# A low-rank-adapted linear layer: VectorE's point of resumption, the last chunk's load, and the placing of two programs

## The chip, the cores and the metric

The kernel runs on one core of one Trainium2 chip. The time is that of the device, in microseconds, for one execution. Five engines run their own instruction streams and meet at semaphores: PE (TensorE, matrix products), DVE (VectorE), ACT (ScalarE), POOL (GpSimd) and SP (SyncE, which here only issues transfers). Transfers between the chip's main memory and the core's on-chip memory (128 partitions) are carried by 16 DMA engines; a transfer that one queue issues is cut into packets that are spread over all 16.

## What is computed

A linear layer with a low-rank addition, on 32,768 rows of 256 numbers:

```
x_flat = x.reshape(-1, in_dim)              # 32768 x 256, fp32
y = x_flat @ W                              # W: 256 x 256
lora_out = x_flat @ lora_A                  # lora_A: 256 x 16
lora_out = lora_out * lora_E
lora_out = lora_out @ lora_B                # lora_B: 16 x 256
y = y + scale * lora_out
return y.reshape(batch, seq_len, out_dim).astype(np.float32)
```

x is 33.55 MB and so is the result; every byte of x is loaded once and every byte of the result stored once.

## The kernel before

The kernel first folds the low-rank part into the weights: `weff = W + A * (E * scale) * B`, kept in bf16. After that the layer is one product, x times `weff`.

**Chunks.** `PLAN` cuts the rows into five chunks: 56, 56, 48, 48 and 48 rows for each of 128 partitions. Three slots in on-chip memory hold them; chunk 3 goes into the slot of chunk 0 and chunk 4 into that of chunk 1. The result overwrites x in the slot, row by row, and a chunk is stored with one transfer when it is finished. `PIECES` says in how many transfers a chunk is loaded: three for chunks 0 and 1, two for chunks 2 and 3, one for chunk 4.

**Steps.** A step t is 8 rows per partition; there are 32. Steps 0 to 6 are chunk 0, 7 to 13 chunk 1, 14 to 19 chunk 2, 20 to 25 chunk 3, 26 to 31 chunk 4. Each step passes through four stages:
- `rounded(t)`, VectorE (L152): 128x2048 numbers of x from fp32 to bf16, into one of two `xb` buffers. It waits for the load of the piece where a piece begins.
- `transposed(k)`, PE (L191): eight transposes into `psum_xt`, with two bf16 numbers moved as one 32-bit word. Each adds to the semaphore `s_t` when the eight are done, so "s_t at 19" means that 19 steps have been transposed.
- `copied(t)`, VectorE (L156): `psum_xt` to on-chip memory.
- `multiplied(k)`, PE (L202): sixteen products of 128x256 into `psum_y`, in two halves; ScalarE evicts each half into the slot (L225).

**Order.** It is written out by hand. VectorE alternates: `copied(t)`, then `rounded(t + 2)`. PE alternates in a loop: the transposes of step t + 1, then the products of step t. So the products of a chunk's last step stand behind the transposes of the next chunk's first step.

**The queue.** All loads and stores of chunks are issued by SP on one queue, in this order: loads 0, 1, 2, then store 0, store 1, load 3, load 4, store 2, store 3, store 4. A load into a slot waits until the store out of it has landed (load 3 for store 0, load 4 for store 1). `ISSUE_STORE` and `ISSUE_LOAD` make some issues wait besides until `s_t` has reached a number: store 1 for 17, load 4 for 19, store 3 for 28. A store also waits for the chunk's last eviction.

**The hold.** `HOLD = 17, 1` keeps VectorE at the rounding of step 17 until store 1 has landed (L147 to L151). Ten NOPs stand in front of that wait:

```
        if t == HOLD[0]:
            for _ in range(10):
                nc.vector.engine_nop()
            nc.vector.wait_ge(s_st[HOLD[1]].sem, 16)
```

The lines that matter later: L104 issues every transfer, L150 is the NOPs, L152 the rounding, L236 and L241 are SP's waits on `s_t`, and the stretch ahead of `opening.append(...)`, where the new alignment goes in.

Of the kernel before, what the change touches and what calls it, by code (L numbers as in the profile page):

```python
# [3 lines left out]

PLAN = [56, 56, 48, 48, 48]

PIECES = {0: [16, 16, 24], 1: [16, 16, 24], 2: [24, 24], 3: [24, 24]}

SLOTS = [56, 56, 48]
LEAD = 3  # L10
AFTER = {1: [3, 4]}

HOLD = 17, 1

ISSUE_LOAD, ISSUE_STORE = {4: 19}, {1: 17, 3: 28}

S, G = 8, 4
P = 128
FP32 = mybir.dt.float32
BF16 = mybir.dt.bfloat16  # L20
# [15 lines left out]
def kernel(tc, x, W, lora_A, lora_B, lora_E, scale, out):  # L36
    nc = tc.nc
    x_flat = x.flatten_outer_dims()
    out_flat = out.flatten_outer_dims()
    N, K = x_flat.shape  # L40
# [14 lines left out]
    def sbuf(name, shape, dt):  # L55
        return nc.alloc_sbuf_tensor(name, shape, dt).ap()
# [9 lines left out]
    b_bf = sbuf("b_bf", [R, M], BF16)  # L66
    ate = sbuf("ate", [R, KC, P], BF16)
    weff = sbuf("weff", [P, KC, M], BF16)
    ident = sbuf("ident", [P, P], FP32)

    xb = [sbuf(f"xb{k}", [P, S, K], BF16) for k in range(2)]
# [13 lines left out]
    for i, b in enumerate(PLAN):  # L85
        parts = PIECES.get(i, [b])
        pieces[i] = [(sum(parts[:j]), n) for j, n in enumerate(parts)]
    s_ld = {(i, r): Count(nc, f"s_ld{i}_{r}") for i in pieces for r, n in pieces[i]}
    s_st = [Count(nc, f"s_st{i}") for i in range(len(PLAN))]
    s_id, s_set, s_v, s_t, s_m, s_y = (  # L90
        Count(nc, k) for k in ("s_id", "s_set", "s_v", "s_t", "s_m", "s_y"))


    can_m = nc.alloc_semaphore("can_m")
# [3 lines left out]
    def slot(i):  # L98
        return slots[i % LEAD][:, :PLAN[i], :]
# [20 lines left out]
        nc.tensor.wait_ge(sem, 1).then_inc(sem, -1)  # L120

    opening.append(tc.info.no_tile_sem_insts)
    transfer(nc.sync, s_w, out=w_sb, in_=W.rearrange("(p c) m -> p c m", c=KC))
# [7 lines left out]
    for i in range(1, LEAD):  # L133
# [5 lines left out]
        out=ident, in_=ident, compare_op=mybir.AluOpType.not_equal, fill=1.0, base=0,  # L139
# [3 lines left out]
    def rounded(t):  # L143
        i, r = steps[t]
        if (i, r) in s_ld:
            nc.vector.wait_ge(s_ld[i, r].sem, 16)
        if t == HOLD[0]:  # L147

            for _ in range(10):
                nc.vector.engine_nop()  # L150
            nc.vector.wait_ge(s_st[HOLD[1]].sem, 16)  # L151
        nc.vector.tensor_copy(out=xb[t % 2], in_=slot(i)[:, r:r + S, :]).then_inc(can_t[t % 2], 1)  # L152

    def copied(t):
# [8 lines left out]
    for c in range(KC):  # L163
# [5 lines left out]
        out=ate, in0=ps_at, scalar1=e_sb, scalar2=float(scale),  # L169
# [6 lines left out]
    nc.vector.wait_ge(s_set.sem, 2)  # L176
    s_v.by(nc.vector.tensor_add(out=weff, in0=w_sb, in1=ps_aeb))  # L177
    rounded(0)
    rounded(1)
    for t in range(NS):  # L180
        copied(t)
        if t + 2 < NS:
            rounded(t + 2)
# [105 lines left out]
```

## Time and profile before

| what | value |
|---|---|
| median of 3 runs | 161.82 us (161.81 to 161.85) |
| the profiled execution, its own time | 161.88 us |
| its span, first to last instruction | 160.6 us |
| bytes moved | 67.42 MB, mean 420 GB/s over the span |
| mean granted TensorE clock | 0.832 |

The transfers on SP's queue, by the trace's records of issue and of landing (each of the 16 DMA engines reports its share; the last report is shown):

| transfer | issued, us | landed, us |
|---|---|---|
| load 0, three pieces | 1.17 to 2.11 | 9.05, 13.95, 21.25 |
| load 1, three pieces | 3.33 to 4.43 | 26.14, 31.04, 38.34 |
| load 2, two pieces | 4.94, 5.43 | 45.65, 53.11 |
| store 0 | 34.66 | 70.44 |
| store 1 | 55.47 | 87.45 |
| load 3, two pieces | 70.46, 70.84 | 94.73, 102.03 |
| load 4, one piece | 94.65 | 116.57 |
| store 2 | 102.67 | 131.06 |
| store 3 | 124.55 | 146.06 |
| store 4 | 140.43 | 160.54 |

How to read it: a transfer is issued long before it lands, because it stands in line behind those issued earlier. The difference between the landings of two neighbours is what the later one needed for itself. The queue would run dry only if a transfer were issued after the one ahead of it had landed. "Span" leaves out 1.3 us that the execution's own time has around the first and last instruction. The page's parts are: engine totals, forty time slices, DMA queues, the chain of waits that ended last, and groups of instructions.

### The profile page before, as it was taken

The numbers are of one execution on the slowest core, as the hardware profiler recorded it, in microseconds if no ns is written. First come the engines' busy times: TensorE is split into PE (matmuls) and PEld (weight loads), VectorE is DVE, ScalarE is ACT, GpSimd is POOL, SyncE is SP. The second block draws the span as 40 slices with busy tenths as digits, with TensorE's granted clock in tenths as the row PEclk, the third lists the DMA queues.
The fourth block names the chain that finished last, engine by engine and source line by source line (L and its number), as shares of the span: only waits on it lengthen the run. The fifth ranks groups of instructions, "written<-read, shape, count | busy, mean of one in ns | idle before, by whom it ended". The sixth has DMA issues, their size and how long they took to land.

```text
span 160.6 us, 1871 instructions
## 1 busy us (share of the span) xinstructions
PE 93.9 (58%) x780; PEld 84.2 (52%) x780; DVE 76.5 (48%) x67; ACT 63.2 (39%) x65; POOL 0.7 (0%) x6
## 2 busy tenths in 40 slices
PE   0159979999999920000000899999569999700000
PEld 0039959999999910000000789999458999500000
DVE  0178679998989300000002968987094985000000
ACT  1101746867777640000000077777605586800000
POOL 1000000000000000000000000000000000000000
PEclk9999999999999997555555599999955999995555
DMA  5999999999999999999998999999999999999994
GB/s 158 426 433 451 435 408 433 449 441 404 459 410 392 457 459 457 457 457 443 443 414 347 404 453 429 435 529 404 404 392 478 465 429 392 416 478 441 416 404 196
DMA packets 2658, 67.42 MB, mean 420 GB/s; under 512 B 464, under 2 KB 480, under 8 KB 608
## 3 DMA queue, kind: packets, MB, share of 16 engines
q1 hardware_dynamic: 2448, 67.37, 97.7%
q10 hardware_dynamic: 208, 0.03, 0.3%
q14 instruction: 2, 0.02, 0.0%
HBM read 33.85 MB, written 33.55 MB: 420 GB/s over the span
## 4 chain that ended last, share of the span: by engine, by line
PE 36%; DMA 34%; DVE 2%; ACT 1%; issue 0%; SPq 0%
PE psum_y L202 23%; DMA out_dram<-xy 20%; DMA xy<-in_x_dram 14%; PE psum_xt L191 13%; DVE xb L152 2%; ACT xy L225 1%; SPq L241 0%; SPq L236 0%
## 5 line engine op out<-in xcount | busy, mean ns | idle before, releaser
L225 ACT COPY xy<-psum_y 128x1024 f32<-128x1024 f32 x64 | 61.9, 1017 | 73.7 <-PE psum_y L202 73.7
L202 PE MATMUL psum_y<-weff,xt 128*128 128x256 bf16 x512 | 64.4, 281 | 0.1
L191 PE MATMUL psum_xt<-ident,xb 128*128 128x128 f32 x264 | 38.1, 293 | 37.9 <-DVE xb L152 37.9
L152 DVE CAST xb<-xy 128x2048 bf16<-128x2048 f32 x32 | 38.9, 1219 | 41.4 <-DMA out_dram<-xy 33.5
L202 PEld LDWEIGHTS psum_y<-weff,xt 128*128 128x128 bf16 x512 | 51.8, 101 | 7.4 <-issue 0.3
L191 PEld LDWEIGHTS psum_xt<-ident,xb 128*128 128x128 f32 x264 | 33.1, 152 | 39.6 <-DVE xb L152 39.2
L156 DVE COPY xt<-psum_xt 128x1024 f32<-128x1024 f32 x32 | 39.1, 1222 | 10.4 <-PE psum_xt L191 10.3
L164 PE MATMUL psum_xt<-ident,a_sb 128*16 128x128 f32 x2 | 0.6, 394 | 4.2 <-POOL ident L138 4.2
L160 DVE CAST b_bf<-b_sb 16x256 bf16<-16x256 f32 x1 | 0.3, 280 | 5.4 <-DMA b_sb<-in_lora_B_dram 5.4
L225 ACT ACT_TABLE_LOAD x1 | 1.3, 1283 | 3.5 <-PEq L132 3.5
L173 PE MATMUL psum_xt<-b_bf,ate 16*128 16x256 bf16 x2 | 0.6, 403 | 3.2 <-DVE ate L168 3.2
L164 PEld LDWEIGHTS psum_xt<-ident,a_sb 128*16 128x16 f32 x2 | 0.1, 90 | 4.2 <-DMA a_sb<-in_lora_A_dram 4.2
L173 PEld LDWEIGHTS psum_xt<-b_bf,ate 16*128 16x128 bf16 x2 | 0.1, 105 | 3.7 <-DVE ate L168 3.7
L168 DVE TENSOR_SCALAR ate<-psum_xt,e_sb 16x256 bf16<-16x256 f32 x1 | 0.5, 471 | 1.8 <-DMA e_sb<-in_lora_E_dram 1.8
L177 DVE TENSOR_TENSOR weff<-w_sb,psum_xt 128x512 bf16<-128x512 f32 x1 | 0.7, 689 | 0.8 <-PE psum_xt L173 0.8
L138 POOL TENSOR_SCALAR_AFFINE_SELECT ident<-ident 128x128 f32<-128x128 f32 x1 | 0.3, 293 | 0.2 <-POOL ident L136 0.2
L136 POOL MEMSET ident<- 128x128 f32 x1 | 0.2, 205 | 2.9 <-POOLq L132 2.9
L270 POOL MEMSET const-bfloat16-1.0<- 128x1 bf16 x1 | 0.1, 102 | 0.0
L270 POOL MEMSET const-uint8-127<- 128x1 uint8 x1 | 0.1, 102 | 0.0
L270 POOL MEMSET const-float32-0.0<- 128x1 f32 x1 | 0.1, 99 | 0.2 <-issue 0.2
L270 POOL MEMSET const-float32-1.0<- 128x1 f32 x1 | 0.1, 99 | 0.0
## 6 DMA issues: line engine op xcount, KB each, us to landing
xy<-in_x_dram SPq DMA_DIRECT2D x6, 3072.0 KB, 32.5
out_dram<-xy SPq DMA_DIRECT2D x3, 6144.0 KB, 21.5
out_dram<-xy SPq DMA_DIRECT2D x2, 7168.0 KB, 33.9
xy<-in_x_dram SPq DMA_DIRECT2D x4, 2048.0 KB, 17.6
xy<-in_x_dram SPq DMA_DIRECT2D x1, 6144.0 KB, 21.9
w_sb<-in_W_dram SPq DMA_DIRECT2D x1, 256.0 KB, 2.8
a_sb<-in_lora_A_dram ACTq DMA_DIRECT2D x1, 16.0 KB, 3.0
b_sb<-in_lora_B_dram ACTq DMA_DIRECT2D x1, 16.0 KB, 4.2
```

The costliest lines, as they stand in the source:

```text
L138: s_id.by(nc.gpsimd.affine_select(out=ident, in_=ident, compare_op=mybir.AluOpType.not_equal, fill=1.0, base=0, pattern=[[-1, P]], channel ...
L152: nc.vector.tensor_copy(out=xb[t % 2], in_=slot(i)[:, r:r + S, :]).then_inc(can_t[t % 2], 1)
L156: nc.vector.tensor_copy(out=xt[t % 2], in_=ps_xt[t % 2]).then_inc(can_m, 1)
L160: s_v.by(nc.vector.tensor_copy(out=b_bf, in_=b_sb))
L164: at_done = nc.tensor.transpose(ps_at[:, c, :], a_sb[:, c, :], ident)
L168: s_v.by(nc.vector.tensor_scalar(out=ate, in0=ps_at, scalar1=e_sb, scalar2=float(scale), op0=mybir.AluOpType.mult, op1=mybir.AluOpType.mult))
L173: aeb_done = nc.tensor.matmul(ps_aeb[:, c, :], ate[:, c, :], b_bf, start=True, stop=True)
L177: s_v.by(nc.vector.tensor_add(out=weff, in0=w_sb, in1=ps_aeb))
L191: done = nc.tensor.transpose(ps_xt[k][:, j, :], words[k][:, j, :], ident)
L202: done = nc.tensor.matmul(ps_y[h][:, j, :], pairs[k][:, h * G + j, :, c], weff[:, c, :], start=(c == 0), stop=(c == KC - 1))
L225: y = nc.scalar.copy(out=slot(i)[:, r:r + G, :], in_=ps_y[h])
L270: nc = _bacc.Bacc("TRN2", target_bir_lowering=False, num_devices=1)
```

## The change

Four things are edited.

1. Chunk 4 is loaded in two pieces of 24 rows, as chunks 2 and 3 are. `rounded` waits for a piece where one begins, so steps 26 to 28 need the first piece and steps 29 to 31 the second.
2. VectorE's hold at step 17 ends when store 0 has landed instead of store 1. Then come four roundings of 16 rows (128x4096 numbers, twice a step's) into a new tile `spare` that nothing reads. After each, VectorE waits for its own semaphore `tick`. The ten NOPs are gone.
3. The numbers of `s_t` that the issues of load 4 and store 3 wait for go up by one, to 20 and 29.
4. VectorE's and ScalarE's instruction streams are each moved, from the place ahead of the first transfers on, to the start of a block of 128 instructions. With `max_nops=0` the gap is jumped over, not filled with instructions to run.

```diff
-PIECES = {0: [16, 16, 24], 1: [16, 16, 24], 2: [24, 24], 3: [24, 24]}
+PIECES = {0: [16, 16, 24], 1: [16, 16, 24], 2: [24, 24], 3: [24, 24], 4: [24, 24]}
...
-HOLD = 17, 1
-
-ISSUE_LOAD, ISSUE_STORE = {4: 19}, {1: 17, 3: 28}
+HOLD = 17, 0, 4
+
+ISSUE_LOAD, ISSUE_STORE = {4: 20}, {1: 17, 3: 29}
...
+    spare = sbuf("spare", [P, 2 * S, K], BF16)
...
+    tick = nc.alloc_semaphore("tick")
...
+    for engine in (nc.vector, nc.scalar):
+        engine.addr_align(128, offset=0, max_nops=0)
...
         if t == HOLD[0]:
-
-            for _ in range(10):
-                nc.vector.engine_nop()
             nc.vector.wait_ge(s_st[HOLD[1]].sem, 16)
+            for _ in range(HOLD[2]):
+                nc.vector.tensor_copy(out=spare, in_=slot(i)[:, r:r + 2 * S, :]).then_inc(tick, 1)
+                nc.vector.wait_ge(tick, 1).then_inc(tick, -1)
         nc.vector.tensor_copy(out=xb[t % 2], in_=slot(i)[:, r:r + S, :]).then_inc(can_t[t % 2], 1)
```

## The prediction

> **What bounds the kernel now.** I read the engine totals and the DMA parts of the page first, then the queue's landings, then the waits of VectorE.
>
> ```profile
> PE 93.9 (58%) x780; PEld 84.2 (52%) x780; DVE 76.5 (48%) x67; ACT 63.2 (39%) x65; POOL 0.7 (0%) x6
> ...
> DMA  5999999999999999999998999999999999999994
> ...
> q1 hardware_dynamic: 2448, 67.37, 97.7%
> ...
> q14 instruction: 2, 0.02, 0.0%
> ```
>
> No compute engine passes 58% and the DMA row reads 9 from the second slice to the last but one: one queue, q1, carries 67.37 MB and its packets fill 97.7% of 16 engines. The reader is to see a kernel whose time is bytes over rate; a compute wait costs only if the queue runs dry. Two packets of another queue, q14, are code.
>
> ```profile
> 87.47 1.23 DVE L152 CAST xb<-xy 128x2048 bf16<-128x2048 f32 x1 [33.46 <-DMA out_dram<-xy]
> ...
> 116.59 1.23 DVE L152 CAST xb<-xy 128x2048 bf16<-128x2048 f32 x1 [5.04 <-DMA xy<-in_x_dram]
> ...
> 138.48 1.93 ACT L225 COPY xy<-psum_y 128x1024 f32<-128x1024 f32 x2 [0.69 <-PE psum_y L202]
> ```
>
> From the timeline: the hold ends at 87.47 after 33.46 us, chunk 4 waits 5.04 us for its load, the last eviction ends at 140.4. None of this starves the queue: store 4 is issued at 140.43 while store 3 drains until 146.06, and store 2 at 102.67 while load 4 drains until 116.57.
>
> So what sets the end lies inside the queue. The trace's packet records give each packet's start, duration and bytes. On every DMA engine they follow one another without a gap and mostly at one duration per size: 912 ns for 24,576 bytes, 1815 for 49,152, 2116 for 57,344. The span ends when the last of 16 engines is done. Their last data ends between 158.62 and 160.06 us, and four deserve a look:
> - Engine C, 160.06: it ends the kernel. From 115.45 to 141.9, while it stores, its packets are 16 to 137 ns longer than 1815, 1105 ns in all. In the same packets the instruction records of all engines number 409; 1105 / 409 = 2.7 ns each, and packet by packet the two rise and fall together (21 records, 61 ns; 40, 104; 50, 137; none, none). While it loads under the same compute it shows 0 to 10 ns. In store 0 it lost 146 ns over 104 records, 1.4 each; through the hold nothing.
> - Engine A, 159.63: at 58.73 a code packet of 8192 bytes ran for 309 ns; engine A paused 302 ns and its next packet was 358 ns too long, 0.66 us.
> - Engine B, 159.47: the same at 108.02, 302 + 380 = 0.68 us.
> - The latest of the other thirteen: 159.20.
>
> **The change, part by part.**
>
> *Resume and spare roundings.* Store 0 lands last at 70.44, so VectorE resumes 17 us sooner. Four roundings of 128x4096 follow; such a size isn't in the trace. The row of half that size takes 1219 ns, or 1130 from start to start back to back: 4 x 2 x 1.13 = 9.0 us at least, 4 x 2 x 1.22 = 9.8 with a full wait after each; I take 9.5, nearer the upper because each waits on its own semaphore. Step 17 is then rounded at 70.46 + 9.5 = 80.0 instead of 87.47. Behind the waiting VectorE stand the transposes of step 17 and ScalarE's evictions; they only come sooner. The spare tile is read by nobody. What moves is when instructions run: store 1 is still on engine C until 86.33, so 6.3 us of steps 17 to 19 now run beside it. The same stretch of the old schedule (87.47 to 93.8) has 63 records; with 8 for the spare roundings and their waits, 71. Price on C: 71 x 1.4 = 0.10 to 71 x 2.7 = 0.19; I take 0.15. The ten NOPs that go took 15 ns each before a wait: nothing, hidden by the 33.46 us.
>
> *Store and load issues.* The issue of load 4 now waits for transpose 20. In the old trace that comes 9.7 us after the resume (97.2 against 87.47), so at about 90; load 3 drains until 102, so the queue is fed. Store 2, behind it on SP's queue, needs the last eviction of chunk 2. That stands after the transposes of step 20, hence after load 3's first piece (94.73): about 101.5, with load 4 draining to 116. Store 3 waits for transpose 29, about 118 to 120 instead of 124.55; store 2 drains to 130. All three cost nothing; if the cover went, each would show as a gap on all 16 engines.
>
> *Two pieces.* Sixteen packets of 24,576 replace eight of 49,152 on each engine. Load 3's pieces repeat every 7.27 us, load 4 took 14.53: 2 x 7.27 = 14.54, and one more semaphore packet of 9 ns: 0.02 us. The first piece lands near 109, the second near 116.6. Step 26 no longer waits 5.04 us. Steps 20 to 25 start at 94.75 after an idle stretch of PE and so at half clock. The old chunk 4 started in that way, and took 9.06 us from its first to its fourth rounding, 2.62 per step later. The same pattern puts rounding 26 at 94.75 + 9.06 + 3 x 2.62 = 111.7. Steps 29 to 31 need the second piece only from 119.5. The last eviction comes near 134 instead of 140.4. Of the 409 records behind 115.45 some 42 then lie in front of it: 3.8 us at 20.7 records per us (39 in a packet of 1.9 us) are some 78, less 36 of step 24's that already lay there. 42 x 2.7 = 0.11 us less on C. If the clock stays up it is up to 0.27, if the pieces land late it is nothing.
>
> *Aligned programs.* [...] At the start the jump may delay ScalarE's three small loads. The bound from below is zero; from above, the queue has load 0 until 20.8 and PE caught up with it at 21.27 (VectorE waited 2.67 us there), so at most some 2 us of steps slip into store 0's window: 40 records x 2.7 = 0.11. I take 0.02, since a code packet took 0.31 us.
>
> [...]
>
> Sum on the engine that ends last: +0.15 - 0.11 + 0.02 + 0.02 = +0.08 us, with ends +0.10 - 0.27 + 0.02 = -0.15 and +0.19 + 0.02 + 0.11 = +0.32. The profiled execution took 161.88 (span 160.6 and 1.3 around it), 0.06 over the median of 161.82. On the median: 161.82 + 0.08 = 161.9.
>
> **Rivals.**
>
> *The handover under compute (slower).* Between 50.2 and 52.8, where load 2 in pieces of 24,576 gives way to store 0 with PE, VectorE and ScalarE busy, 14 packets were 55 to 484 ns too long: the mean over 16 engines lost about 0.29 us. Where load 4 in packets of 49,152 gave way to store 2 at 115, with PE idle, the mean lost 0.03. After the change that handover has small packets and busy engines, like the first one. If either decides it, all engines lose about 0.3: 161.9 + 0.3 = 162.2. It decides from the point where engine C is among those hit. Against it: at 50 us C itself had no long packet, and one event does not make a rule.
>
> *Engine C's slowness is not in the timed runs (faster).* If the 2.7 ns per instruction come from recording the profile, the timed runs end with engine A, and the aligned programs take its 0.66 us: 159.63 becomes 159.20 + 0.02, so 161.82 - 0.41 = 161.4. For it: only one DMA engine suffers, in step with the count of records. Against it: a timed run without the loss should lie 160.06 - 159.63 = 0.43 below the profiled execution, and it lies 0.06 below. [...]
>
> *The alignment doesn't do what it says.* The code packets stay in the span at other times. If they hit A and B again: 161.9. If one hit C: 161.9 + 0.67 = 162.6. Both old ones missed C.
>
> **How the numbers follow.** The forecast gets 0.50, the handover 0.25, the faster rival 0.20, the alignment 0.05 (0.03 as forecast, 0.02 at 162.6). A measurement here tells about 0.2%, 0.32 us, from no change. Faster needs less than 161.50, which only the faster rival gives: 0.20. Slower needs more than 162.14: the handover and 162.6 give 0.27, and the forecast's upper end (161.82 + 0.32) just touches it, 0.01: 0.28. Same: 0.52. The likeliest case alone spans 161.67 to 162.14. To hold 8 in 10 I take in the faster rival's 161.4 and the handover's 162.2 with a little around them, 161.35 to 162.3.
>
> **What would show it.** In the changed profile: a rounding into the spare tile at 70.5 and step 17 near 80; no wait of 5 us before step 26; the last eviction near 134; q14 without packets inside the span, and so engines A and B among the others; engine C still last, with longer packets in store 1 and fewer long ones behind 115. The forecast is wrong if the DMA row shows a gap, if the packets near 115 are longer on all engines, or if C no longer ends last.

## The result and the profile after

The change made the kernel slower. The median of 22 runs is 162.50 us against 161.96 for the kernel before (22 runs), a ratio of 1.0030 with a 95% interval of 1.0021 to 1.0038: 0.5 us, 0.34 to 0.6. The profiled execution took 162.25 us, span 160.9, which is near the fast end of its 22 runs (162.21 to 162.98); that of before lies at the fast end of its own. So the two traces show 0.37 us of the 0.5.

First the DMA part of the page of the changed kernel:

```profile
DMA  5999999999999999999997999999999999999993
...
q1 hardware_dynamic: 2592, 67.37, 97.9%
...
q14 instruction: 2, 0.02, 0.1%
```

The queue is as full as before, 97.9%. There are still two code packets on q14 in the span, and they took more, 0.1% instead of 0.0%. The packet records put them at 1.76 (1016 ns) and 2.84 us (309 ns), no longer at 58.7 and 108.0. With the alignments both stand in the opening.

What they do there stands in the timeline of the first 30 us and in the list of transfers (its last column is the time from issue to landing, in us). In the kernel before:

```profile
0.74 0.40 ACTq L104 DMA_DIRECT2D a_sb<-in_lora_A_dram  x1
...
9.32 2.36 DVE L152 CAST xb<-xy 128x2048 bf16<-128x2048 f32 x2
```

```profile
a_sb<-in_lora_A_dram ACTq DMA_DIRECT2D x1, 16.0 KB, 3.0
```

In the changed kernel:

```profile
1.16 2.78 ACTq L106 DMA_DIRECT2D a_sb<-in_lora_A_dram  x1
...
13.30 0.59 PE L169 MATMUL psum_xt<-ident,a_sb 128*16 128x128 f32 x2 [13.30 <-DMA a_sb<-in_lora_A_dram]
...
17.79 2.35 DVE L157 CAST xb<-xy 128x2048 bf16<-128x2048 f32 x2
```

```profile
a_sb<-in_lora_A_dram ACTq DMA_DIRECT2D x1, 16.0 KB, 12.1
b_sb<-in_lora_B_dram ACTq DMA_DIRECT2D x1, 16.0 KB, 10.3
e_sb<-in_lora_E_dram ACTq DMA_DIRECT2D x1, 0.1 KB, 11.5
```

ScalarE's first load was issued in 0.40 us at 0.74 before; now the instruction is open for 2.78 us. When it gets through, 16 engines are busy with x, and 16 KB need 12.1 us instead of 3.0. PE waits for them until 13.30 (4.2 before), and the first rounding comes at 17.79 instead of 9.32.

VectorE in the middle and the last eviction, from the timeline:

```profile
70.87 9.61 DVE L155 CAST spare<-xy 128x4096 bf16<-128x4096 f32 x4 [10.32 <-DMA out_dram<-xy]
80.62 1.23 DVE L157 CAST xb<-xy 128x2048 bf16<-128x2048 f32 x1
...
95.00 1.23 DVE L157 CAST xb<-xy 128x2048 bf16<-128x2048 f32 x1 [5.67 <-DMA xy<-in_x_dram]
...
131.52 1.93 ACT L230 COPY xy<-psum_y 128x1024 f32<-128x1024 f32 x2 [0.69 <-PE psum_y L207]
```

The four spare roundings take 9.61 us, step 17 starts at 80.62, step 20 waits for load 3 until 95.00, and the last eviction ends at 133.4. That part went by plan.

Where PE works beside which transfer can be read from the view by windows. The windows are store 0, store 1, loads 3 and 4, and the stretch in which stores 2 and 3 run; the first columns are the window's length and PE's busy time with its matmuls. The kernel before:

```profile
52.30:69.40 17.10, 4.82 (x45) 4.18 (x42) 1.46 (x2) 4.53 (x5) 0.00 (x0) 0.80 1.04 450
69.40:86.30 16.90, 0.00 (x0) 0.00 (x0) 0.00 (x0) 0.00 (x0) 0.00 (x0) 0.50 0.96 417
...
115.50:141.00 25.50, 21.44 (x168) 19.10 (x168) 15.29 (x13) 13.85 (x15) 0.00 (x0) 0.87 1.00 434
```

and the changed one:

```profile
52.30:69.40 17.10, 11.35 (x104) 10.28 (x102) 7.46 (x7) 9.64 (x10) 0.00 (x0) 0.91 1.03 444
69.40:86.30 16.90, 4.40 (x21) 3.59 (x22) 14.85 (x9) 0.69 (x1) 0.00 (x0) 0.50 0.97 421
...
115.50:141.00 25.50, 16.86 (x155) 15.40 (x152) 11.31 (x10) 13.50 (x14) 0.00 (x0) 0.88 1.01 435
```

PE works 6.5 us more beside store 0, 4.4 more beside store 1 and 4.6 less beside stores 2 and 3. Engine C again ends last: 160.39 us, 0.34 later. The sums of its packets' excess over the usual duration, with the instruction records that fell into them:

| beside | before: ns, records | after: ns, records | difference, us |
|---|---|---|---|
| store 0 | 146, 104 | 491, 230 | +0.345 |
| store 1 | 0, 2 | 144, 66 | +0.144 |
| stores 2 to 4 | 1119, 410 | 993, 382 | -0.126 |

The three make +0.36. (The last row has the few ns behind 141.9 us too, which the prediction left out.) Loads 3 and 4 add 0.10 (29.12 us on engine C before, 29.22 after), and engine C entered store 0 0.12 earlier; together that is the 0.34. The next engine ends at 159.98, and it is neither A nor B as they were: before store 0 three engines are 0.6 to 0.8 us behind the middle of the 16 (load 2's first piece ends at 45.37, 45.38 and 45.55 on them, near 44.8 in the middle), and behind the handover 0.8 to 1.1. The lag is there from load 0 on, so they were left behind in the opening. So two things had come with the alignment: late small loads, and engines left behind.

### The profile page after: what moved, and what is told of

The parts are those of the page before. It is cut to its first block, busy times and chain, and to the rows that moved or that the text cites. A ratio compares the mean times of both kernels' runs of the same rounds, so it can differ in the third digit from the quotient of the medians.

```text
span 160.9 us, 1874 instructions
## 1 busy us (share of the span) xinstructions
PE 92.3 (57%) x780; PEld 82.7 (51%) x780; DVE 85.6 (53%) x71; ACT 63.2 (39%) x65; POOL 0.7 (0%) x6
## 3 DMA queue, kind: packets, MB, share of 16 engines
q1 hardware_dynamic: 2592, 67.37, 97.9%
## 5 line engine op out<-in xcount | busy, mean ns | idle before, releaser
L196 PE MATMUL psum_xt<-ident,xb 128*128 128x128 f32 x264 | 36.6, 286 | 24.1 <-DVE xb L157 24.1
L196 PEld LDWEIGHTS psum_xt<-ident,xb 128*128 128x128 f32 x264 | 31.9, 148 | 25.6 <-DVE xb L157 25.1
L155 DVE CAST spare<-xy 128x4096 bf16<-128x4096 f32 x4 | 9.2, 2294 | 10.8 <-DMA out_dram<-xy 10.3
## 6 DMA issues: line engine op xcount, KB each, us to landing
a_sb<-in_lora_A_dram ACTq DMA_DIRECT2D x1, 16.0 KB, 12.1
```

The lines of the kernel that those rows point to most:

```text
L155: nc.vector.tensor_copy(out=spare, in_=slot(i)[:, r:r + 2 * S, :]).then_inc(tick, 1)
L196: done = nc.tensor.transpose(ps_xt[k][:, j, :], words[k][:, j, :], ident)
```

## The experiments

All are compared with the kernel before on the same chip; us are the ratio's distance from 1 times 162.

**1. The alignments, together and one by one, and the change without them.** The kernel before with the lines below (`align_only`), or with one engine of the two (`align_scalar`, `align_vector`):

```diff
+    for engine in (nc.vector, nc.scalar):
+        engine.addr_align(128, offset=0, max_nops=0)
     opening.append(tc.info.no_tile_sem_insts)
```

> The kernel before with the two alignments and nothing else. Theory (late small loads): ScalarE waits for its code behind the jump, its three small loads then stand behind the 16 engines' full load of x, the weights are folded some 8 us later, and about 6 us more of steps run beside store 0 on DMA engine C, at 2.2 to 2.7 ns per instruction record: engine C loses about 0.5 us in store 0 instead of 0.15, the time goes up by 0.3 to 0.5 us, nearly all of what the whole change cost. Rival (VectorE's earlier resumption beside store 1, or the split, costs it): alignment alone changes nothing or gains, 0 to -0.2 us.

> The kernel before with ScalarE's alignment alone. Theory (late small loads): as with both, +0.3 to +0.5 us; the first small load lands after 10 us; one code packet stays inside the span late. Rival (any jump at the start costs, or VectorE's does): half of it or less, up to +0.2 us.

> The kernel before with VectorE's alignment alone. Theory (late small loads): VectorE has nothing to issue at the start and its jump is done before the small loads land, so PE still starts near 4 us, the first rounding stays near 9.3 us, and the time moves by less than 0.15 us. Rival (VectorE's late code is what delays the start): the first rounding several us later, +0.3 to +0.5 us.

`after_no_align` is the changed kernel without those two lines.

> The changed kernel without the two alignments: resumption, spare roundings, split and issue numbers stay. Theory (late small loads): the first rounding is back near 9.3 us; engine C loses 0.14 us beside store 1 and gains 0.12 us behind 115 us, so -0.05 to +0.15 us against the kernel before. Rival (the resumption or the split costs it): +0.3 to +0.5 us still.

| kernel | ratio (95%) | us |
|---|---|---|
| both alignments alone | 1.0026 (1.0013 to 1.0038) | +0.42 |
| ScalarE's alone | 1.0030 (1.0012 to 1.0049) | +0.49 |
| VectorE's alone | 0.9997 (0.9986 to 1.0008) | -0.05 |
| the change without them | 1.0015 (0.9997 to 1.0032) | +0.24 |

The timeline of the opening, first with ScalarE's alone, then with VectorE's alone:

```profile
1.16 2.87 ACTq L104 DMA_DIRECT2D a_sb<-in_lora_A_dram  x1
...
17.14 2.35 DVE L153 CAST xb<-xy 128x2048 bf16<-128x2048 f32 x2
```

```profile
0.74 0.41 ACTq L104 DMA_DIRECT2D a_sb<-in_lora_A_dram  x1
...
9.31 2.36 DVE L153 CAST xb<-xy 128x2048 bf16<-128x2048 f32 x2
```

ScalarE's jump does all of it: 2.87 us against 0.41, and the first rounding 8 us late. VectorE jumps without harm to the time: nothing at the start waits for it. The two runs also show whose code the packets inside the span of the kernel before were: with ScalarE aligned one stays at 65.22 us, with VectorE aligned one stays at 108.07. So the one at 58.74 was VectorE's and the one at 108.02 ScalarE's. The change without the alignments lies between "nothing" and the whole, with an interval too wide to place it better.

But the traces of the aligned kernels held something that the theory did not have. With ScalarE's alone an engine other than C ended last: it was 0.8 us behind before store 0 and had one packet of load 2 that was 1184 ns too long at 50.95 us. With both, one such packet at 51.31 was 1697 ns too long, and its engine ended last as well. VectorE's alignment left an engine behind too, by 0.56 us; it came out of the handover 0.67 behind and ended at 159.66, hidden behind engine C at 160.22. That led to runs 3 and 4.

**2. What engine C pays for.** GpSimd executes 200 NOPs in a loop, behind store 0, while store 1 drains and nothing else works.

```diff
+    nc.gpsimd.wait_ge(s_st[0].sem, 16)
+    with nc.gpsimd.Fori(0, 50):
+        for _ in range(4):
+            nc.gpsimd.engine_nop()
+    nc.gpsimd.sem_inc(nopped, 1)
```

> The kernel before with 200 NOPs (and some 100 instructions of their loop) on GpSimd while store 1 drains and every other engine waits; they read and write no tensor. Theory (engine C pays per recorded instruction while it stores): engine C's packets of store 1, which are at 2116 ns without them, become longer by 300 records x 1.4 to 2.7 ns = 0.4 to 0.8 us in all, the other 15 engines stay, and the time goes up by 0.4 to 0.8 us. Rival (engine C pays for the tensors that compute engines read and write): nothing, 0.

Measured: 1.0050 (1.0032 to 1.0068), +0.8 us. Seven packets of store 1 on engine C, from 71.49 to 86.96 us, became 80 to 113 ns longer, 680 ns over 284 records: 2.4 ns each. Engine C ended at 160.70 instead of 160.06; packets of that stretch on the other engines did not lengthen. NOPs touch no tensor, so it is the instructions, or the recording of them, that engine C pays for, not the data. And all six runs pay it, not the profiled one alone. Each run's record has spans and clocks, so none is known to have run without recording; whether such an execution would pay it stays open.

The other side of it: the four spare roundings read 8 MB through VectorE in 9.6 us in the changed kernel, and engine C's packets beside them grew by 24 ns in all.

**3. The small loads on time, the alignments kept.** Once by putting the two lines behind ScalarE's three loads (`align_behind_small`), once by letting SP issue the three between load 0's first and second piece (`small_on_sp`).

> The changed kernel with both alignments moved behind the issue of the three small loads. Theory (late small loads): the small loads land near 4 to 7 us as in the kernel before, the first rounding stays near 9.3 us, and the code packets still come at the start: 0.3 to 0.5 us below the changed kernel, within 0.1 us of the kernel before. Rival (the jump itself or the rest of the change costs it): as the changed kernel, +0.3 to +0.5 us against before.

> The changed kernel with both alignments, but the three small loads issued by SP behind load 0's first piece instead of by ScalarE. Theory (late small loads): they land near 8 to 9 us, the first rounding comes near 11 to 12, PE has caught up by 21 us, engine C loses about 0.15 us in store 0 again: 0.2 to 0.4 us below the changed kernel. Rival (a code packet early in the span leaves one DMA engine 0.6 us behind, and that engine then loses more where load 2 gives way to store 0): +0.3 to +1.0 us against before, with the last engine another than C.

Measured 1.0062 (1.0049 to 1.0075), +1.0 us, and 1.0041 (1.0024 to 1.0058), +0.67. Both misses for the theory of the small loads alone. The first rounding was at 9.43 and 12.05 us, so the compute was on time, and the kernels were still slower. In both an engine other than C ended last, at 161.70 and 160.64; it was 0.9 and 0.8 us behind before the handover at 50 us, and there had a packet that was 1142 and 1194 ns too long. In the first kernel it lost another 1.1 us where load 4 gave way to store 2. All six traces with a code packet in the first 7 us have at least one engine 0.56 to 1.16 us behind at load 2's first piece; in the others, but for `lag_early` below, no engine is more than 0.31 behind. That the engine left behind is the one that carried the code is inferred. What it then loses at the handover is the question of run 4.

**4. An engine left behind by other means.** ScalarE issues two extra loads of 16 KB into a tile that nothing reads. Each puts one packet of 8192 bytes, the size of a code packet, on each of two engines. `lag_early` has the 17 below, `lag_late` 57 in its place.

```diff
+        if n == 17:
+            for u in range(2):
+                transfer(nc.scalar, s_x, out=scrap[:, u, :], in_=x_flat[16 * u:16 * u + 16, :].rearrange("(p a) k -> p (a k)", p=2))
```

> The kernel before with two extra transfers of 16 KB (8 KB on each of two DMA engines, as the code packets have) issued by ScalarE near 25 us, while loads run; what they bring is not used. They put two engines some 0.7 to 1.3 us behind. Theory (an engine that is behind loses more at the handover from load 2 to store 0): those engines are another 0.5 us or more behind after 53 us, and one of them ends last: +0.7 us or more. Rival (being behind is only carried along): they end at 159.2 + 0.7 to 1.3, so 0 to +0.5 us.

> The same two extra transfers issued near 125 us, when only stores are left. Both theories: two engines 0.7 to 1.3 us behind and nothing that adds to it, 0 to +0.5 us (up to +1.3 if one of them is engine C).

They were issued later than the expectations say, the early ones at 37.67 us instead of near 25 (scrap is the tile). The early ones, then the late ones:

```profile
37.67 0.76 ACTq L106 DMA_DIRECT2D scrap<-in_x_dram  x2
```

```profile
129.55 0.98 ACTq L106 DMA_DIRECT2D scrap<-in_x_dram  x2
```

Early: 1.0049 (1.0030 to 1.0068), +0.8 us. Two engines were 0.8 and 1.2 us behind at 45 us; two packets at the handover were 992 and 1536 ns too long (0.1 to 0.5 us is what others lost there), and the two engines came out 1.3 and 2.2 us behind. They ended at 160.89 (that one met a code packet at 109.5 too, 0.6 us) and 161.14, and the latter ended the kernel. Late: 1.0006 (0.9992 to 1.0019). Here the extra packets put the two engines only 0.6 us behind. One of them had carried a code packet at 108.26 as well and was 1.22 behind in all; with no more loads to come it stayed at 1.22 and ended at 160.28, before engine C (160.38). The extra loads are no code, so here being 0.8 and 1.2 us behind was enough for an engine to lose more at the handover, 1.0 and 1.5 us in one packet.

How much more differs. The table has every engine that was more than 0.5 us behind, against the middle of the 16, at the end of load 2's first piece and at the start of store 0; each row is one execution.

| kernel | behind at 45 us | behind at the start of store 0 |
|---|---|---|
| `align_vector` | 0.56 | 0.67 |
| `align_only` | 0.57, 1.16 | 0.57, 2.09 |
| changed | 0.59, 0.60, 0.77 | 0.81, 0.82, 1.05 |
| `small_on_sp` | 0.71, 0.76 | 0.89, 1.28 |
| `align_scalar` | 0.80 | 1.31 |
| `align_behind_small` | 0.89 | 1.56 |
| `lag_early` | 0.83, 1.18 | 1.29, 2.19 |

A lag of up to 0.77 us grew by 0 to 0.5, a lag of 0.8 to 1.2 by 0.5 to 1.0. It does not grow at every handover: where load 4 gave way to store 2, the latest engines of `align_only` and `lag_early`, 2.1 and 2.2 us behind, lost nothing more, while in `align_behind_small` 1.5 became 2.6. What decides this stays open.

**5. The late small loads alone.** `small_late` is the kernel before with no alignment; SP issues the three loads between load 0's second and third piece.

> The kernel before with no alignment, no code packet moved, and the three small loads issued by SP behind load 0's second piece, so that they land near 13 us as in the changed kernel. Theory (two costs): the delay alone puts some 5 us more of steps beside store 0 and costs engine C about 0.3 us, so +0.2 to +0.4 us, with no engine behind from the start. Rival (only the engine left behind by an early code packet matters): 0 to +0.1 us.

Measured 1.0018 (1.0009 to 1.0027), +0.3 us. The first rounding came at 16.13. Engine C lost 435 ns in store 0 and ended last at 160.54; no engine was behind. The window of store 0 has PE at 10.1 us:

```profile
52.30:69.40 17.10, 10.12 (x93) 9.11 (x91) 6.23 (x6) 8.43 (x9) 0.00 (x0) 0.90 1.02 440
```

So each of the two effects costs by itself, 0.3 us and 0.7 to 1.0. They don't add up, because the later of two engines sets the end.

**6. The other parts alone.**

`hold_only` has the changed kernel's `HOLD`, the loop of spare roundings behind it and no NOPs, `split_only` its `PIECES`; each is otherwise the kernel before.

```diff
-HOLD = 17, 1
+HOLD = 17, 0, 4
...
-PIECES = {0: [16, 16, 24], 1: [16, 16, 24], 2: [24, 24], 3: [24, 24]}
+PIECES = {0: [16, 16, 24], 1: [16, 16, 24], 2: [24, 24], 3: [24, 24], 4: [24, 24]}
```

> The kernel before with the resumption behind store 0 and the four spare roundings alone (no split, no alignment, old issue numbers, no NOPs). Theory: engine C pays 0.10 to 0.19 us for steps 17 to 19 beside store 1, nothing for the spare roundings themselves; chunk 4 still waits for its whole load: +0.1 to +0.2 us. Rival (the earlier resumption pays off): 0 or below.

> The kernel before with chunk 4's load in two pieces alone. Theory: chunk 4's steps start about 5 us sooner, 40 to 100 instruction records move from beside store 2 to beside load 4, and engine C gains 0.1 to 0.27 us: -0.1 to -0.27 us. Rival (the handover from small packets to a store under busy engines costs all 16 engines about 0.3 us): 0 to +0.2 us.

The resumption: 1.0008 (1.0000 to 1.0017), +0.13 us, as worked out, though the interval touches 1. The split: 1.0000 (0.9991 to 1.0009). In its trace step 26 was rounded at 111.63, where the prediction had put it, but engine C still lost 1066 ns beside stores 2 to 4 instead of 1119: only 30 records left the stretch (380 instead of 410), fewer than the 40 to 100 expected. And the 16 engines had lost 0.76 us on the mean at the first handover instead of 0.25, ahead of anything that the split touches; the earliest of them ended at 158.86 instead of 158.61. Whether the split is worth 0.1 us stays open; 0.27 is excluded.

**7. Fewer instructions beside stores.** If the price per record holds, a schedule that keeps up with loads 3 and 4 should win. `early_fine` drops the hold and the NOPs and cuts load 3 into 8, 16, 24 rows and load 4 into 24, 16, 8. `flow_8` and `flow_16` keep the resumption behind store 0 and cut more finely.

> The kernel before without its hold and its NOPs, and with load 3 in pieces of 8, 16 and 24 rows and load 4 in pieces of 24, 16 and 8. Theory (engine C pays 2.7 ns per instruction record beside a store): steps 17 to 19 move beside store 0 and cost 0.3 to 0.4 us there, but steps 20 to 31 run from about 89 to 122 us and leave some 150 instead of 409 records behind 115 us, 0.7 us less; engine C then ends with engine A: -0.2 to -0.4 us. Rival (the handover under busy engines, or small pieces, cost all engines): 0 to +0.3 us.

> The kernel before with the resumption behind store 0 and the spare roundings, and loads 3 and 4 in six pieces of 8 rows each. Theory (2.7 ns per record beside a store, and no engine behind): steps 20 to 31 follow the loads from 89 us on and end near 126 instead of 140; some 200 instead of 409 records lie behind 115 us, -0.55 us, steps 17 to 19 beside store 1 cost +0.15: -0.2 to -0.45 us. Rival (smaller pieces or the handover under busy engines cost all engines): 0 to +0.4 us.

> As flow_8, with load 3 in pieces of 8, 8, 16, 16 rows and load 4 in 16, 16, 8, 8. Theory: as flow_8, the steps about one step later: -0.15 to -0.4 us. Rival: 0 to +0.4 us.

| kernel | ratio (95%) | engine C beside stores 2 to 4: ns, records | earliest engine ends, us |
|---|---|---|---|
| before | 1 | 1119, 410 | 158.61 |
| early_fine | 1.0025 (1.0015 to 1.0035) | 895, 316 | 158.73 |
| flow_8 | 1.0030 (1.0018 to 1.0043) | 662, 229 | 159.19 |
| flow_16 | 1.0015 (1.0006 to 1.0024) | 733 in the seven longest packets, some 265 | 158.89 |

All slower. In `early_fine` the schedule did not come out as planned: step 23 stood until 24 rows had landed, so only 94 records left the stretch, and steps 17 to 19 cost 0.39 us beside store 0. In `flow_8` it did, the last eviction ended at 126.9, and the window shows PE at half its work there:

```profile
115.50:141.00 25.50, 10.33 (x95) 9.33 (x93) 5.38 (x5) 8.65 (x10) 0.00 (x0) 0.79 1.02 439
```

Engine C got back 0.46 us, and 229 records cost 2.9 ns each, so the price held. But loads 3 and 4 took every engine some 0.5 us longer in packets of 8192 bytes (29.6 us from the end of store 1 to that of load 4, 29.1 before). What was gained on one engine was paid on 16. (In the single traces the first handover adds to this: it took 0.5 us on the mean in all three, 0.25 before.) None of the runs beats the kernel before.

## Why the prediction was wrong

The step that failed is the last part of the change, "At the start the jump may delay ScalarE's three small loads", priced at 0.02 us with 0.11 as the upper bound. It cost 0.345 on engine C in the trace. The bound came from PE having caught up with load 0 at 21.27 us in the old trace. That was right for a delay of 2 us: in `small_on_sp` the first rounding came 2.7 us late, and engine C lost 194 ns in store 0 instead of 146. The delay was 8.5, because I took the length of the code packet (0.31 us) for the time that the issue would lose (2.78 us less 0.40, 2.4) and did not ask what the late loads would then stand behind: 16 engines full of x. With 8.5 us PE catches up nowhere before store 0: the first wait of VectorE for a load of x is the one before 95.00.

Inside the span ScalarE lost nothing by its code packet: in the kernel before its evictions around 108.02 started at 105.96 and 108.58, 2.62 us apart like other steps. The DMA engine that carried the code lost 0.68 us.

Engines left behind were not in the sum either. In the changed kernel engines are left 0.6 to 0.8 us behind in the opening, and that was not carried along unchanged, but grew at the handover from load 2 to store 0. In the traced execution it grew by some 0.25 us and stayed hidden behind engine C; in `align_only`, `align_scalar` and the kernels of run 3 by 0.5 to 0.9 us on the engine that then ended last. So "the aligned programs take its 0.66 us", from which the 161.4 is worked out, was my estimate, and no run shows it: the packets left 58.7 and 108.0 us, but all six traces with a code packet in the first 7 us have an engine 0.56 to 1.16 us behind. Whether the growth at the handover is why the median of the changed kernel lies 0.25 above its traced execution was not seen, since only one execution of it has a trace.

Right were:
- what bounds the kernel, and that engine C ends last. Its price per record held: 2.1 to 2.2 ns beside stores 0 and 1 (1.4 to 2.7 predicted), 2.6 beside stores 2 to 4;
- the resumption: 9.61 us for the spare roundings (9.5), step 17 at 80.62 (80.0), +0.144 us beside store 1 (+0.15), and +0.13 (0 to 0.28) by itself;
- chunk 4, in part by luck: -0.126 us (-0.11), with step 26 at 110.83 (111.7) and the last eviction at 133.4 (134). Only 28 records left the stretch, not 42, at 2.6 ns for each that stayed instead of 2.7; in `split_only` 30 left and 0.05 us was gained;
- the issues of loads and stores: nothing.

Of the rivals, the handover under busy engines did not come where it was placed: around 115 us single packets of three engines of the changed kernel were too long, by 30, 63 and 153 ns. "Not in the timed runs" fell with the NOPs, whose ratio of 1.0050 is one of timed runs; whether recording is what costs there too is not shown. That the alignment does other than it says was half right: the code packets stayed in the span at other times, 1.76 and 2.84 us, but the price set for it (0.67 on engine C) was not what it cost.

## What to carry to other kernels

Where one queue keeps all DMA engines full (97.7% here), look at the engines one by one. Here the last of 16 ended the kernel, and small things on one engine (a code packet, 0.66 and 0.68 us on its engine; two 16 KB loads at 37.67 us, +0.8 us on the kernel; 284 recorded instructions beside store 1, +0.8) were worth more than VectorE's wait of 33.46 us, whose earlier end gained nothing (+0.13 in `hold_only`). Before moving an engine's code, list what that engine issues first and what these transfers will stand behind when they come a few us later. Check a delay against the whole chain, up to the first place where somebody waits anyway, with the delay's own length (2.4 us here) rather than a code packet's (0.31).

## What the runs showed of the hardware

- While engine C, one of the 16 DMA engines, stored, its packets were longer by 2.1 to 2.9 ns for each recorded instruction of the core's engines, NOPs included (1.4 beside store 0 of the kernel before); 284 in a stretch without any other work cost 680 ns there (`pool_nops`), and that kernel took 0.8 us more. Whether executing or recording them costs it was not found.
- DMA engines that were 0.8 and 1.2 us behind the others lost more where load 2 gave way to store 0: they came out 1.3 and 2.2 behind in `lag_early`, while 0.57 stayed 0.57 in `align_only`. Where load 4 gave way to store 2, 2.2 stayed 2.2. What they wait for there was not found.
- At the handover from load 2 to store 0 the 16 engines lost 0.2 to 0.8 us on the mean in the 17 traces, and it differs also where nothing ahead of it was changed: 0.25 in the kernel before, 0.76 in `split_only`. So a difference below 0.5 us between two single traces cannot be read from their ends alone; it has to be followed stretch by stretch.
- With ScalarE's stream aligned ahead of its first load, the issue of that load took 2.78 us (changed kernel), 2.87 (`align_scalar`) and 3.10 (`align_only`), against 0.40 in the kernel before and 0.41 in `align_vector`. The two code packets of 8192 bytes in the opening of the changed kernel took 1016 and 309 ns, the two inside the span of the kernel before 309 each. What the issue waits for was not shown.
